# Mem's norm factors from squares of mem^T on GpSimd and two small matmuls, in place of a block of mem squared on ScalarE

## The chip, the core and the metric

The kernel runs on one core of a Trainium2 chip. The metric is the device time of one execution in microseconds (us), lower is better. A core has TensorE (PE, with its weight loads PEld), VectorE (DVE), ScalarE (ACT), GpSimd (POOL) and SyncE (SP), which issues most of the DMAs. Each engine runs its own instructions in order and waits for the others by semaphores.

## What is computed

A trunk of two layers over 256 tokens of width 1024. Each layer normalizes its input, projects it, runs 12 self-attention heads (layer 0 with forget gates, layer 1 with ALiBi) and 4 cross-attention heads into 256 fixed memory tokens `mem`, adds the output projection, and runs a SwiGLU feed-forward block (FFN). Shapes: `x` and `mem` (1, 256, 1024), all float32. What matters here is the part on `mem`:

```
def rms_norm(x, g):
    y = x * lax.rsqrt(jnp.mean(x * x, axis=-1, keepdims=True) + RMS_EPS)
    return y * g

for i in range(2):
    xn = rms_norm(h, norm_mix[i])
    mn = rms_norm(mem, norm_mem[i])
    mkv = mn @ w_mem_kv[i]
    mk, mv = split_heads(mkv[..., :256], 4), split_heads(mkv[..., 256:], 4)
    proj = xn @ (w_in_fox[0] if i == 0 else w_in_moba[0])      # q, k, v, gates (i == 0), qm
    ...
    mem_out = memory_attention(qm, mk, mv)
    ...
```

The factor of a memory token, one over the root of its mean square, is the same in both layers.

## The kernel before

All weights come as one stream of blocks of up to 1 MB, [128 partitions, 2048 columns], in the order in which `Plan` lists them. `fetch` loads the next block into one of four `raw` buffers; `split` makes of half a block at a time a rounded part `hi` (ScalarE, line 215) and a rest `lo` (VectorE, line 216), so that three matmuls (hi x hi, lo x hi, hi x lo; `prod`) stand for one of full precision. Each use of a half splits five halves ahead, and each split fetches up to three blocks ahead.

`x` and `mem` come transposed into the same stream (`xT`, `memT`): channel on the partition, token on the column, eight slices k of 128 channels. `split_x` makes `x_x` and `x_mem` of them, with the gain applied (line 237 on ScalarE, line 238 on VectorE). The norm factors per token aren't needed for the matmuls; they are applied to their results. For that, before the change, `mem` comes a second time, as a block of its own with the token on the partition (`U["mem"]`): `mem_kv(0)` squares it on ScalarE with a running sum (`mean_square`, line 243), adds epsilon on VectorE (`me_mem`, line 254), raises to -1/2 on GpSimd (`rs_mem`, line 256), and `spread` makes a row of the factors for all partitions with four matmuls (`rsb_ps_mem`) and a copy (`rsb_mem`, line 267).

PE's and SP's instructions go out in the order in which the program lists them (`manual_schedule`); those of VectorE, ScalarE and GpSimd are put in order by a planner that runs while the program is built. That program order in layer 0: values and gates (`v_ps`); q and k of the first four heads (`qk_ps`, g = 0); then `memory_heads`: keys and values of the memory tokens (`mk_ps`, `mv_ps`; eight slices k, "mkv" below), the memory queries (`qm_ps`, eight slices k), and q and k of the next heads (g = 1, 2). Attention of a pair of heads is a generator (`attend`) that `step()` moves on between the slices: `s_m` and `s_s` are the scores of memory and self heads, `p_m` and `p_s` the probabilities. `split_queries` and `split_keys` make the operands `xq`, `xk`, `mk`, `xqm` from the scaled products, on ScalarE, VectorE and GpSimd.

`gate_sums` makes the running sums of the gates: two products, a copy `fr`, a DMA to memory (`fd`, line 490) and three DMAs that spread it over all partitions (`fk`, line 493). `bias` makes from `fk` the additive bias of a pair of self heads (line 510). PSUM banks (eight) and the `work` tiles are shared in turn.

Of the kernel before, what the change touches and what calls it, by code (L numbers as in the profile page):

```python
# [20 lines left out]
F32 = mybir.dt.float32  # L21
# [3 lines left out]
ALU = mybir.AluOpType  # L25
# [3 lines left out]
P = 128  # L29
D = 1024  # L30
S = 256
# [47 lines left out]
class Plan:  # L79


    def __init__(self, a):
        self.shapes, self.blocks, self.U = [], [], {}
        U = self.U
        xT = np.ascontiguousarray(a["x"][0].T)
        memT = np.ascontiguousarray(a["mem"][0].T)
        U["xT"] = self.unit([xT], 0, KD, 0, S)
        for i in range(2):
            w = a["w_in_fox"][0] if i == 0 else a["w_in_moba"][0]
            nv = SW + (H if i == 0 else 0)  # L90
            U["vf", i] = []
            for u in range(4):
                U["vf", i].append(self.unit([w], 2 * u, 2, 2 * SW, nv))
            for g in range(3):
                if g == MEM_AT[i]:
                    if i == 0:
                        U["memT", 0] = self.unit([memT], 0, KD, 0, S)
                        self.mkv(a, 0)
                        self.blocks.append(a["mem"][0].reshape(NT, P, D).transpose(1, 0, 2).reshape(-1))
                        self.shapes.append((NT, 1, D))  # L100
                        U["mem"] = len(self.shapes) - 1
                    U["qm", i] = self.unit([w], 0, KD, 2 * SW + nv, MW)
                U["qk", i, g] = [self.unit([w[:, :SW], w[:, SW:]], 4 * u, 4, g * 2 * P, 2 * P) for u in range(2)]
            U["out", i] = [self.unit([a["w_out"][i]], 2 * j, 2, 0, D) for j in (3, 0, 1, 2)]
            U["gu", i], U["dn", i] = {}, {}
            wgu = a["w_gate_up"][i]
            for c in range(NFC):
                U["gu", i][c, 0] = self.gate_up(wgu, 2 * c)
                if c == NFC - 1:
                    U["gu", i][c, 1] = self.gate_up(wgu, 2 * c + 1)  # L110
                if c > 0:
                    U["dn", i][c - 1] = self.unit([a["w_down"][i]], 2 * (c - 1), 2, 0, D)
                if c < NFC - 1:
                    U["gu", i][c, 1] = self.gate_up(wgu, 2 * c + 1)
            U["dn", i][NFC - 1] = self.unit([a["w_down"][i]], 2 * (NFC - 1), 2, 0, D)
            if i == 0:
                U["memT", 1] = self.unit([memT], 0, KD, 0, S)
                self.mkv(a, 1)
# [20 lines left out]
def trunk(ctx: ExitStack, tc: tile.TileContext, plan, stream, x, gains, norm_final, b_fgate, square, out):  # L139
# [40 lines left out]


    U = plan.U
    raw_only = {U["xT"], U["memT", 0], U["memT", 1], U["mem"]}
    halves = [(i, j * (sh[0] // 2), sh[0] // 2) for i, sh in enumerate(plan.shapes) if i not in raw_only for j in range(2)]
    starts = np.concatenate([[0], np.cumsum([P * int(np.prod(sh)) for sh in plan.shapes])])
    ready, raws, counts = {}, {}, [0, 0]
# [100 lines left out]
    def split_x(i, gain, dst, ks=range(KD)):  # L287

        fetch_to(i + 1)
        for k in ks:  # L290
            split_ps(dst[0][:, k, :], dst[1][:, k, :], raws[i][:, k, 0, :], gT[:, k, gain:gain + 1])
# [28 lines left out]
    rs_mem = []  # L320
    rsb_mem = []

    def mem_kv(i):

        xs = xposed(f"mem{i}")
        split_x(U["memT", i], 2 + i, xs, range(MEM_AHEAD))
        yield
        kb, vb = bank(f"mk_ps{i}"), bank(f"mv_ps{i}")
        for u in range(2):
            for kk in range(4):  # L330
                wh, wl = weights(U["mkv", i][u], kk)
                k = 4 * u + kk
                mv_ = (xs[0][:, k, :], xs[1][:, k, :])
                if k + MEM_AHEAD < KD:
                    split_x(U["memT", i], 2 + i, xs, (k + MEM_AHEAD,))
                for p in range(HM // 2):
                    c = slice(p * P, (p + 1) * P)
                    prod(kb, kb.t[:, p * S:(p + 1) * S], (wh[:, 0, c], wl[:, 0, c]), mv_, k == KD - 1)
                for t in range(NT):
                    c = slice(MW, 2 * MW)  # L340
                    prod(vb, vb.t[:, t * S:(t + 1) * S], tok(xs, k, t), (wh[:, 0, c], wl[:, 0, c]), k == KD - 1)
                if kk % 2:
                    yield
        if i == 0:
            fetch_to(U["mem"] + 1)
            rs_mem.extend(factor(raws[U["mem"]][:, t, 0], f"mem{t}") for t in range(NT))
            rsb_mem.append(spread(rs_mem, "mem", (1.0,), "mem")[:, 0, :])
        mk = ap.tile([P, HM // 2, S], F32, tag="work", name=f"mk{i}", bufs=WORK_BUFS)
        nc.vector.tensor_mul(mk, kb.t.rearrange("p (a s) -> p a s", a=2), rsb_mem[0].unsqueeze(1).to_broadcast([P, 2, S]))
        for p in range(HM // 2):  # L350
            split_keys(mks[p], mk[:, p])
        for t in range(NT):
            nc.scalar.activation(mvs[t][:, :, 0:DH], vb.t[:, t * S:(t + 1) * S].rearrange("p (a d) -> p a d", d=DH),
                                 AF.Copy, scale=rs_mem[t])
# [4 lines left out]
    def split_queries(dst, q):  # L359

        for a in range(2):
            nc.scalar.activation(dst[HOME[a], a], q[HOME[a]], AF.Copy)  # L362
        for a in range(2):
            ENG[a].tensor_sub(dst[HOME[1 - a], a], q[HOME[a]], dst[HOME[a], a].bitcast(F32))

    def split_keys(dst, k):

# [63 lines left out]
        yield  # L431

    active = []

    def step():
        for g in list(active):
# [4 lines left out]
    def mixer(i, xs, rs):  # L441
# [41 lines left out]
        def gate_sums():  # L483
            yield
            fb = bank("F_ps")
            fb.mm(fb.t[:H, 0:S], lf[:, 0], prefix)
            fb.mm(fb.t[:H, P:S], lf[:, 1], prefix[:, 0:P], stop=True)
            fr = ap.tile([P, 2, S], F32, tag="work", name="fr", bufs=WORK_BUFS)[:H, 0]
            nc.vector.tensor_copy(fr, fb.t[:H, :S])
            nc.sync.dma_start(fd, fr)  # L490
            for g in range(GATE_PARTS):
                hs = slice(g * (H // GATE_PARTS), (g + 1) * (H // GATE_PARTS))
                nc.sync.dma_start(fk[:, hs], fd[hs].unsqueeze(0).to_broadcast([P, H // GATE_PARTS, S]))
            gb = bank("Fq_ps")
            for t in range(NT):
                for u in range(t + 1):
                    gb.mm(gb.t[:, t * H:(t + 1) * H], prefix[:, (t - u) * P:(t - u + 1) * P], lf[:, u], stop=u == t)
            nc.scalar.activation(fq.rearrange("p t h -> p (t h)"), gb.t[:, :NT * H], AF.Copy)

        def bias(h0):  # L500

            b = fk[:, h0:h0 + 2]
            if i == 1:
                for a in range(2):
                    nc.gpsimd.tensor_scalar(b[:, a], dist, -float(slopes[h0 + a]), NEG, op0=ALU.mult, op1=ALU.max)
                return b[:, :, P:], b
            b0 = ap.tile([P, 2, P], F32, tag="bias", name=f"bias{h0}", bufs=1)
            for a in range(2):
                for t, o in ((0, b0), (1, b)):
                    nc.vector.scalar_tensor_tensor(o[:, a], b[:, a, :(t + 1) * P], fq[:, t, h0 + a:h0 + a + 1], mask[:, P - t * P:],  # L510
                                                   op0=ALU.subtract, op1=ALU.add)
            return b0, b

        hT = xposed(f"hT{i}")
# [2 lines left out]
        def memory_heads():  # L517
            if i == 0:
                g = mem_kv(0)
                next(g)  # L520
                for j in range(4):
                    next(g)
                    step()
            qb = bank(f"qm_ps{i}")
            for k in range(KD):
                wh, wl = weights(U["qm", i], k)
                for p in range(HM // 2):
                    c = slice(p * P, (p + 1) * P)
                    prod(qb, qb.t[:, p * S:(p + 1) * S], (wh[:, 0, c], wl[:, 0, c]), (xs[0][:, k, :], xs[1][:, k, :]), k == KD - 1)
                if k == 3:  # L530
                    step()
            if i == 0:
                next(g, None)
            qm = ap.tile([P, 2, S], F32, tag="work", name=f"qm{i}", bufs=WORK_BUFS)
            nc.vector.tensor_mul(qm, qb.t.rearrange("p (a s) -> p a s", a=2), rsb[:, 0:1, :].to_broadcast([P, 2, S]))
            for p in range(HM // 2):
                xq = ap.tile([P, 2, S], F32R, tag="work", name=f"xqm{i}{p}", bufs=WORK_BUFS)
                split_queries(xq, qm[:, p])
                active.append(attend(f"m{i}{p}", xq, mks[p], mvs, 2 * p, IDLE_MEM[i] + p, None, hT, 6 + p))

        for g in range(3):
# [245 lines left out]
```

## Time and profile before

| | |
|---|---|
| median of three runs | 627.83 us (625.1 to 628.57) |
| the profiled execution's own time | 628.3 us |
| its span, first to last instruction | 626.5 us |
| busy PE, PEld, DVE, ACT, POOL | 97, 86, 73, 63, 10% |
| mean granted TensorE clock | 0.992 of full speed |
| DMA | 112.31 MB, 179 GB/s |

In the rows, a time in front is the start in us from the span's first instruction; an operation is written out<-in by the program's names, without buffer numbers; x2 means that two were merged into one row, with the time from the first one's start to the last one's end. L216 is line 216 of the kernel. `SPq` is SP's issue of a DMA. "[0.9 <-PE x]" is idle time of the engine ahead of the row and what ended it.

### The profile page before, as it was taken

To read this page: it belongs to the slowest core of one execution; us is meant where nothing else is said; L and a number is where in the kernel's file an instruction comes from. 1 tells how busy PE (TensorE), PEld (TensorE's weight loads), DVE (VectorE), ACT (ScalarE), POOL (GpSimd) and SP (SyncE) were. 2 spreads that over 40 slices of the span, in tenths; PEclk is the share of its full clock that TensorE was granted. 3 is DMA by queue.
4 is the path that set the end of the run, shared out by engine and by line. 5 is a ranking of instruction groups with operands and counts; after the bars stand their busy time and mean duration, and the time that the engine had idled before them with its cause. 6 is when DMAs were issued, how large, how long until landed. Compare 5 with 4: busy or idle time off the path is not lost.

```text
span 626.5 us, 9569 instructions
## 1 busy us (share of the span) xinstructions
PE 609.5 (97%) x3636; PEld 536.2 (86%) x3636; DVE 457.3 (73%) x827; ACT 392.6 (63%) x734; POOL 60.4 (10%) x90
## 2 busy tenths in 40 slices
PE   7999899999999999999999999999999999999995
PEld 5999887778888888888899999877888888888884
DVE  5588899978676666668675589986876666676664
ACT  6679887666555555557466589875755555555542
POOL 2021345300000000000011033100000000000000
PEclk8999899999999999999999999999999999999999
DMA  8974812445555555555555633332455545555301
GB/s 293 390 283 166 347 69 85 146 173 202 199 174 179 194 196 202 194 177 176 210 186 194 215 140 126 135 134 68 169 201 202 186 176 181 198 201 202 136 0 67
DMA packets 17638, 112.31 MB, mean 179 GB/s; under 512 B 2220, under 2 KB 2744, under 8 KB 5432
## 3 DMA queue, kind: packets, MB, share of 16 engines
q1 hardware_dynamic: 17304, 111.42, 49.1%
q8 instruction: 28, 0.46, 0.3%
q10 hardware_dynamic: 288, 0.29, 0.1%
q14 instruction: 18, 0.15, 0.1%
HBM read 110.64 MB, written 1.06 MB: 178 GB/s over the span
## 4 chain that ended last, share of the span: by engine, by line
PE 83%; DVE 7%; ACT 6%; issue 2%; DMA 2%; POOL 0%; SPq 0%; POOLq 0%; ACTq 0%; DVEq 0%
PE gu L178 39%; PE d_acc L178 18%; PE qk_ps L178 8%; PE v_ps L178 6%; PE o_acc L178 4%; DVE lo L216 2%; DMA raw<-in_stream 2%; ACT hi L215 2%; PE s_s L178 1%; ACT p_s L406 1%; PE mv_ps L178 1%; PE qm_ps L178 1%; PE mk_ps L178 1%; PE s_m L178 1%; ACT xq L362 1%
## 5 line engine op out<-in xcount | busy, mean ns | idle before, releaser
L216 DVE TENSOR_TENSOR lo<-raw,hi 128x1024 fp32r<-128x1024 f32 (+3 forms) x201 | 240.6, 1204 | 70.6 <-ACT hi L215 65.6
L215 ACT ACTIVATE hi<-raw 128x1024 fp32r<-128x1024 f32 (+3 forms) x201 | 206.2, 1034 | 74.2 <-PE d_acc L178 47.0
L178 PE MATMUL gu<-x_ffn,hi 128*128 128x512 f32 x704 | 177.5, 392 | 0.0
L178 PEld LDWEIGHTS gu<-x_ffn,hi 128*128 128x128 f32 x704 | 126.3, 189 | 22.2
L178 PE MATMUL d_acc<-hi,h 128*128 128x512 f32 x348 | 107.1, 389 | 0.0
L178 PEld LDWEIGHTS gu<-x_ffn,lo 128*128 128x128 f32 x704 | 96.7, 190 | 8.1 <-ACT x_ffn L237 1.0
L178 PE MATMUL gu<-x_ffn,lo 128*128 128x256 f32 x704 | 100.5, 284 | 0.2
L178 PEld LDWEIGHTS d_acc<-hi,h 128*128 128x128 f32 x348 | 65.3, 188 | 13.6
L178 PE MATMUL qk_ps<-x_x,hi 128*128 128x256 f32 x384 | 73.7, 288 | 0.0
L178 PE MATMUL d_acc<-lo,h 128*128 128x512 f32 x174 | 67.7, 389 | 0.0
L178 PEld LDWEIGHTS qk_ps<-x_x,hi 128*128 128x128 f32 x384 | 62.1, 195 | 0.8 <-issue 0.8
L178 PE MATMUL qk_ps<-x_x,lo 128*128 128x256 f32 x192 | 55.0, 286 | 0.0
L642 ACT ACTIVATE gate<-gu 128x256 f32<-128x256 f32 x44 | 16.9, 384 | 57.6 <-PE gu L178 57.6
L178 PE MATMUL o_acc<-hi,x_hT 128*128 128x512 f32 x128 | 41.7, 404 | 0.6 <-DVE x_hT L235 0.3
L642 ACT ACTIVATE up<-gu 128x256 f32<-128x256 f32 x44 | 16.9, 385 | 40.0 <-PE gu L178 39.7
L178 PEld LDWEIGHTS d_acc<-lo,h 128*128 128x128 f32 x174 | 32.7, 188 | 6.8
L178 PEld LDWEIGHTS qk_ps<-x_x,lo 128*128 128x128 f32 x192 | 37.6, 196 | 0.0
L643 DVE TENSOR_TENSOR gate<-gu,gate 128x256 f32<-128x256 f32 x44 | 18.7, 424 | 25.8 <-ACT gate L642 25.8
L643 DVE TENSOR_TENSOR up<-gu,up 128x256 f32<-128x256 f32 x44 | 18.7, 425 | 25.1 <-ACT up L642 25.1
L178 PE MATMUL v_ps<-hi,x_x 128*128 128x384 f32 (+1 forms) x128 | 34.3, 350 | 1.7 <-ACT hi L215 1.7
L406 ACT ACTIVATE p_s<-p_s,nmax_s 128x128 f32<-128x128 f32 (+1 forms) x48 | 21.4, 446 | 11.8 <-DVE nmax_s L396 11.6
L178 PEld LDWEIGHTS o_acc<-hi,x_hT 128*128 128x128 f32 x128 | 22.8, 188 | 6.4 <-issue 1.3
(152 smaller groups left out, 752.3 us busy)
## 6 DMA issues: line engine op xcount, KB each, us to landing
raw<-in_stream SPq DMA_DIRECT2D x95, 1024.0 KB, 4.8
raw<-in_stream SPq DMA_DIRECT2D x4, 768.0 KB, 4.5
raw<-in_stream SPq DMA_DIRECT2D x2, 780.0 KB, 8.3
fk<-fd SPq DMA_DIRECT2D x3, 512.0 KB, 4.9
raw<-in_stream SPq DMA_DIRECT2D x3, 390.0 KB, 6.2
h<-in_x SPq DMA_DIRECT2D x2, 512.0 KB, 7.1
raw<-in_stream SPq DMA_DIRECT2D x1, 512.0 KB, 7.1
gfin<-in_norm_final SPq DMA_DIRECT2D x1, 512.0 KB, 3.7
```

Of the source, the lines that this page charges most:

```text
L178: nc.tensor.matmul(o, lhsT, rhs, start=self.fresh, stop=stop, skip_group_check=True)
L215: nc.scalar.activation(hi[:, c0:c1], src[:, c0:c1], AF.Copy)
L216: nc.vector.tensor_sub(lo[:, c0:c1], src[:, c0:c1], hi[:, c0:c1].bitcast(F32))
L362: nc.scalar.activation(dst[HOME[a], a], q[HOME[a]], AF.Copy)
L406: nc.scalar.activation(pr[:, a, c], src, AF.Exp, bias=nmax[:, a, j], scale=scale, accum_out=total[:, a, j])
L642: nc.scalar.activation(v[:, 1], b[s].t[:, S:], AF.Copy)
L643: nc.vector.tensor_add(v[:, 0], b[s].t[:, :S], v[:, 1])
```

## The change

The block `mem` leaves the stream. In its place GpSimd squares the eight slices of `memT` and adds them up (`mem_squares`), and two matmuls with a column of -1 sum over the partitions, token by token (`mem_factors`); the same two steps on VectorE and GpSimd as before make the factors. These matmuls are issued after slice k = 1 of the memory queries, and `spread` with the scaling of `mk` and `mv` after k = 4 instead of behind all eight. Further: the three DMAs of `fk` are issued two steps later, and the instructions of `bias` are kept behind the last VectorE instruction of the second pair's `split_queries` (`issue_after`: an order on the same engine, no wait).

```
-                        self.blocks.append(a["mem"][0].reshape(NT, P, D).transpose(1, 0, 2).reshape(-1))
-                        self.shapes.append((NT, 1, D))
-                        U["mem"] = len(self.shapes) - 1
...
-    raw_only = {U["xT"], U["memT", 0], U["memT", 1], U["mem"]}
+    raw_only = {U["xT"], U["memT", 0], U["memT", 1]}
...
+    def mem_squares():
+        w = cp.tile([P, 2, S], F32, name="squares")
+        for k in range(KD):
+            src = raws[U["memT", 0]][:, k, 0, :]
+            nc.gpsimd.tensor_mul(w[:, min(k, 1)], src, src)
+            if k > 0:
+                nc.gpsimd.tensor_add(w[:, 0], w[:, 0], w[:, 1])
+        return w[:, 0]
+
+    def mem_factors(sums):
+        b = bank("ms_mem")
+        for t in range(NT):
+            b.mm(b.t[:, 2 * t:2 * t + 2], sums[:, t * P:(t + 1) * P], prefix[:, P:P + 2], stop=True)
+        for t in range(NT):
+            me = sp.tile([P, 1], F32, tag="me", name=f"me_mem{t}")
+            nc.vector.tensor_scalar(me, b.t[:, 2 * t:2 * t + 1], -1.0 / D, EPS, op0=ALU.mult, op1=ALU.add)
+            rs = sp.tile([P, 1], F32, tag="rs", name=f"rs_mem{t}", bufs=8)
+            nc.gpsimd.tensor_tensor(rs, me, minus_half, op=ALU.pow)
+            rs_mem.append(rs)
+
     def mem_kv(i):
         xs = xposed(f"mem{i}")
         split_x(U["memT", i], 2 + i, xs, range(MEM_AHEAD))
+        if i == 0:
+            sums = mem_squares()
         yield
...
         if i == 0:
-            fetch_to(U["mem"] + 1)
-            rs_mem.extend(factor(raws[U["mem"]][:, t, 0], f"mem{t}") for t in range(NT))
+            mem_factors(sums)
+            yield
             rsb_mem.append(spread(rs_mem, "mem", (1.0,), "mem")[:, 0, :])
...
     (split_queries)
         for a in range(2):
-            ENG[a].tensor_sub(dst[HOME[1 - a], a], q[HOME[a]], dst[HOME[a], a].bitcast(F32))
+            r = ENG[a].tensor_sub(dst[HOME[1 - a], a], q[HOME[a]], dst[HOME[a], a].bitcast(F32))
+        return r
...
+    mem_done = {}
...
     (gate_sums)
             nc.sync.dma_start(fd, fr)
-            for g in range(GATE_PARTS):
-                hs = slice(g * (H // GATE_PARTS), (g + 1) * (H // GATE_PARTS))
-                nc.sync.dma_start(fk[:, hs], fd[hs].unsqueeze(0).to_broadcast([P, H // GATE_PARTS, S]))
...
             nc.scalar.activation(fq.rearrange("p t h -> p (t h)"), gb.t[:, :NT * H], AF.Copy)
+            yield
+            yield
+            for g in range(GATE_PARTS):
+                hs = slice(g * (H // GATE_PARTS), (g + 1) * (H // GATE_PARTS))
+                nc.sync.dma_start(fk[:, hs], fd[hs].unsqueeze(0).to_broadcast([P, H // GATE_PARTS, S]))
...
     (bias)
-                    nc.vector.scalar_tensor_tensor(o[:, a], b[:, a, :(t + 1) * P], fq[:, t, h0 + a:h0 + a + 1], mask[:, P - t * P:],
-                                                   op0=ALU.subtract, op1=ALU.add)
+                    with tc.issue_after(mem_done[i]):
+                        nc.vector.scalar_tensor_tensor(...)
...
     (memory_heads, in the loop over k of qm)
+                if i == 0 and k in (1, 4):
+                    next(g, None)
                 if k == 3:
                     step()
-            if i == 0:
-                next(g, None)
...
-                split_queries(xq, qm[:, p])
+                mem_done[i] = split_queries(xq, qm[:, p]).ins
```

## Rows read from the trace of the kernel before

**Rows 1.** The page: busy time and share of the span of each engine, and the chain that ended last by engine.

```profile
PE 609.5 (97%) x3636; PEld 536.2 (86%) x3636; DVE 457.3 (73%) x827; ACT 392.6 (63%) x734; POOL 60.4 (10%) x90
PE 83%; DVE 7%; ACT 6%; issue 2%; DMA 2%; POOL 0%; SPq 0%; POOLq 0%; ACTq 0%; DVEq 0%
```

**Rows 2.** What PE waited for between 40 and 130 us: us in total, times, longest.

```profile
PE s_m L178 <- POOL xqm L364: 2.0, 1, 2.0
...
```

**Rows 3.** The chain that ended last, in order of time (start us, us, what), around that wait.

```profile
...
54.26 5.95 DMA raw<-in_stream
...
66.06 1.22 PE s_m L178 x8
67.28 4.37 PE qk_ps L178 x24
...
72.61 0.94 PE s_m L178 x8
73.56 2.88 PE qk_ps L178 x24
...
```

**Rows 4.** The two squares of mem on ScalarE (line 243) between 40 and 60 us: count, ns min/median/max, first and last start.

```profile
L243 ACT ACTIVATE junk_mem<-raw x2: 1043/1045/1047, 50.2 to 53.1; 128x1024 bf16<-128x1024 f32 x2
```

**Rows 5.** Busy time in some stretches: stretch, its length, then busy us (instructions) of PE, PEld, DVE, ACT, POOL, the granted clock, the DMAs' share and GB/s.

```profile
65.00:70.00 5.00, 3.94 (x22) 3.94 (x23) 4.66 (x10) 4.87 (x11) 1.51 (x2) 0.71 1.04 418
...
85.00:113.00 28.00, 25.99 (x177) 20.75 (x174) 27.33 (x72) 22.58 (x55) 12.24 (x14) 1.00 0.29 110
```

**Rows 6.** VectorE's two `lo` of the qm block (timeline of VectorE), SP's issues of `fd` and `fk` (timeline of SP).

```profile
49.27 2.36 DVE L216 TENSOR_TENSOR lo<-raw,hi 128x1024 fp32r<-128x1024 f32 x2 [1.10 <-ACT hi L215]
...
54.64 0.44 SPq L490 DMA_DIRECT2D fd<-fr  x1
60.39 1.29 SPq L493 DMA_DIRECT2D fk<-fd  x3
```

**Rows 7.** Timeline of PE at the start of mkv, at the start of qm, and at the end of qm with the start of the next q and k.

```profile
38.96 0.28 PE L178 MATMUL mk_ps<-x_mem,lo 128*128 128x256 f32 x1
...
51.97 0.28 PE L178 MATMUL qm_ps<-x_x,hi 128*128 128x256 f32 x1
...
57.73 0.60 PE L178 MATMUL rsb_ps_mem<-sq,rs_mem 128*128 128x128 f32 x4
58.09 0.36 PE L178 MATMUL qk_ps<-x_x,hi 128*128 128x256 f32 x1
```

**Rows 8.** SP's issue of memT's block, and the time from its issue to its landing.

```profile
16.89 0.33 SPq L198 DMA_DIRECT2D raw<-in_stream  x1
...
DMA to landing us min/median/max: 13.9/13.9/13.9
```

**Rows 9.** Timeline of GpSimd: from 20 to 43 us, and at 88 us.

```profile
22.47 1.24 POOL L256 TENSOR_TENSOR rs_x<-me_x,minus_half 128x1 f32<-128x1 f32 x2 [17.67 <-DVE me_x L254]
42.03 1.60 POOL L364 TENSOR_TENSOR xq<-qk,xq 64x256 fp32r<-64x256 f32 x1 [18.32 <-ACT xq L362]
...
88.49 1.71 POOL L364 TENSOR_TENSOR xq<-qk,xq 64x256 fp32r<-64x256 f32 x1 [2.07 <-ACT xq L362]
```

**Rows 10.** Timelines of VectorE and GpSimd where both have two-input instructions, at 88, 108 and 384 us (VectorE's rows first in each).

```profile
88.39 1.22 DVE L216 TENSOR_TENSOR lo<-raw,hi 128x1024 fp32r<-128x1024 f32 x1
89.64 0.84 DVE L364 TENSOR_TENSOR xq<-qk,xq 64x256 fp32r<-64x256 f32 x1
...
108.26 1.65 DVE L216 TENSOR_TENSOR lo<-raw,hi 128x1024 fp32r<-128x1024 f32 x1
...
108.08 0.74 POOL L372 TENSOR_TENSOR xk<-qk,xk 64x256 fp32r<-64x256 f32 x1 [0.15 <-ACT xk L369]
...
383.70 0.55 DVE L410 TENSOR_SCALAR p_m<-p_m,rc_m 128x256 f32<-128x256 f32 x1
...
384.17 0.88 DVE L410 TENSOR_SCALAR p_m<-p_m,rc_m 128x256 f32<-128x256 f32 x1
...
384.18 0.72 POOL L372 TENSOR_TENSOR xk<-qk,xk 64x256 fp32r<-64x256 f32 x1
```

**Rows 11.** GpSimd's one-input instruction `fk<-sq` (line 505): all twelve, ns min/median/max; two of them in GpSimd's timeline, and VectorE's `lo` under them.

```profile
L505 POOL TENSOR_SCALAR fk<-sq x12: 1066/1070/1916, 73.6 to 119.3; 128x256 f32<-128x256 f32 x12
...
96.34 2.47 POOL L505 TENSOR_SCALAR fk<-sq 128x256 f32<-128x256 f32 x2 [2.18 <-issue]
...
96.67 1.22 DVE L216 TENSOR_TENSOR lo<-raw,hi 128x1024 fp32r<-128x1024 f32 x1
```

**Rows 12.** Timeline of VectorE from 30 to 39 us.

```profile
30.77 2.36 DVE L216 TENSOR_TENSOR lo<-raw,hi 128x1024 fp32r<-128x1024 f32 x2 [0.76 <-ACT hi L215]
33.05 3.25 DVE L238 SCALAR_TENSOR_TENSOR x_mem<-raw,gT,x_mem 128x256 fp32r<-128x256 f32 x8
36.22 2.35 DVE L216 TENSOR_TENSOR lo<-raw,hi 128x1024 fp32r<-128x1024 f32 x2
```

**Rows 13.** Timelines of GpSimd and VectorE around the last `xqm`, and the first reader of `bias` on VectorE.

```profile
65.28 1.60 POOL L364 TENSOR_TENSOR xqm<-qm,xqm 64x256 fp32r<-64x256 f32 x2 [1.07 <-ACT xqm L362]
...
66.32 0.85 DVE L510 SCALAR_TENSOR_TENSOR fk<-fk,fq,sq 128x256 f32<-128x256 f32 x1
67.20 0.42 DVE L364 TENSOR_TENSOR xqm<-qm,xqm 64x256 fp32r<-64x256 f32 x1
...
72.17 0.29 DVE L396 CUSTOM_DVE_ANT_0 p_s<-s_s,bias 128x128 f32<-128x128 f32 x1 [0.91 <-PE s_s L178]
```

More of the change, by code (lines that the diff above doesn't have):

```diff
@@ L509, in bias @@
                 for t, o in ((0, b0), (1, b)):
-                    nc.vector.scalar_tensor_tensor(o[:, a], b[:, a, :(t + 1) * P], fq[:, t, h0 + a:h0 + a + 1], mask[:, P - t * P:],
-                                                   op0=ALU.subtract, op1=ALU.add)
+                    with tc.issue_after(mem_done[i]):
+                        nc.vector.scalar_tensor_tensor(o[:, a], b[:, a, :(t + 1) * P], fq[:, t, h0 + a:h0 + a + 1],
+                                                       mask[:, P - t * P:], op0=ALU.subtract, op1=ALU.add)
             return b0, b
```

## The prediction, made before the changed kernel was run

> **What bounds the kernel now.** I read the page first: PE (TensorE) is busy 97% of the span and makes 83% of the chain that ended last [rows 1]. So a change counts only where it makes PE wait, or ends a wait. The view of PE's waits over the stretch in which mem's factors are made shows where it waits [rows 2]: one wait of 2.0 us is by far the longest, `s_m` (scores of the first memory pair) for `xqm` on GpSimd. The chain in order of time says where that came from [rows 3]: a raw block issued at 54.26 landed 5.95 us later, ScalarE stood in its order at that block's `hi`, and the `mk` and `xqm` copies came behind it, so that `s_m` began at 66.06. The reader should see in ScalarE's own rows that the two squares of mem (1.05 us each) stand ahead of this [rows 4], and that the block's issue at 54.26 comes right behind the second (53.1 + 1.05 and the reading of its sum): the buffer that mem's block held is the one it waited for. After the wait the granted clock falls [rows 5]: 0.71 on average in 65 to 70 us, that is, half (1.2 GHz) for a part of it. The chain prices it: `s_m` took 1.22 us where the next pair took 0.94, and 24 `qk_ps` matmuls took 4.37 us where the next 24 took 2.88 [rows 3]. So the wait costs 1.98, and the low clock behind it 0.28 + 1.49 = 1.77: together 3.75 us.
>
> From 85 to 113 us VectorE is the fuller engine (27.33 of 28 us) and the chain runs through it, but it is fed by `s_s`, `s_m` and `qk`, and it had idled 0.91 us when `s_s` gave it `p_s` at 72.17 [rows 13]: it had no backlog then, so a shift of PE there is passed on. The FFN stages behind do not change.
>
> **The change, removed.** The 1 MB mem block, one place in the stream with four buffers; two squares on ScalarE, 2 x 1.05 = 2.1 us. The last `qk` block no longer waits for a square: its buffer is qm's, free when qm's second `lo` ends at about 51.6 [rows 6], so with the same 6 us it would land near 57.7, ahead of 60.29. ScalarE has 2.1 us less to do and no block to wait for ahead of 66.06, more than the 1.98 that `s_m` lacked. The factors also move: `spread` is issued after k = 4 of qm, not after k = 7, three steps of six matmuls at 0.12 us (2.2 us) earlier than its neighbours. I take the whole 3.75 us as gained; the floor is nothing (rival 3).
>
> **Added on PE.** Two matmuls of two columns. Four of `rsb_ps_mem` took 0.36 us (57.73 to 58.09) [rows 7]; two cost 0.2. Nothing covers them, PE is the bound.
>
> **Added on GpSimd.** Fifteen instructions, eight products and seven sums, each 128x256 with both inputs in SBUF. They can start when memT lands: issued at 16.89, 13.9 us to landing, 30.8 [rows 8]. GpSimd is empty from 23.7 to 42.03 [rows 9]. No row shows a two-input GpSimd instruction on 128 partitions; the nearest are `xq`/`xk`, 64x256, 0.72 us undisturbed, and `fk<-sq`, 128x256 with one input, 1.07 [rows 10, 11]. Alone the fifteen would take 15 x 0.8 = 12 us (with 0.08 between) to 17 and be done by 43 to 48, long before PE has done k = 1 of qm (51.97 + 12 x 0.12 = 53.4 [rows 7]). So GpSimd's own time is covered, even when doubled.
>
> What isn't covered is VectorE. The rows of the two engines side by side show that a two-input GpSimd instruction and a VectorE instruction with two inputs in SBUF take turns [rows 9, 10]. `xq` on GpSimd began at 88.49 under a `lo` that ended at 89.61, and ended at 90.20, 0.59 later; VectorE's `xq`, begun at 89.64, took 0.84 where the like `xqm` at 67.20 took 0.42 alone [rows 13]. A `lo` begun at 108.26 under GpSimd's `xk` took 1.65 for 1.22. And where both have more to do, GpSimd gets the next turn: of VectorE's two `p_m` at 383.70 and 384.17 the second took 0.88 while GpSimd's `xk`, begun at 384.18, took its undisturbed 0.72. The Trainium skill says the same of these ports ("SBUF — State Buffer", Who interferes with whom): the pair is an exclusive lock, held for a whole instruction, and the loser blocks fully. The trace agrees for two-input GpSimd instructions; it does not for the one-input `fk<-sq` at 96.34, under which a `lo` at 96.67 took its plain 1.22 [rows 11]; by the rule that `lo` would have been held.
>
> Now where the fifteen fall. From 30.77 VectorE does two `lo`, eight `x_mem` and two `lo` without a gap, all with two SBUF inputs [rows 12]. With turns, a GpSimd instruction comes before each:
> - second `lo`: 0.59 + 1.09 (the `lo` of 108.26 ended 1.09 after GpSimd's end at 108.82) = 1.68 instead of 1.14: +0.54;
> - eight `x_mem`: 0.59 + 0.29 (the like form `fk` at 66.32 ended 0.29 after GpSimd [rows 13]) = 0.88 instead of 0.40: +3.84;
> - the third `lo`: +0.54.
> Sum +4.9 us. The third `lo` is the first half of mkv's weights. It ended at 36.22 + 1.22 = 37.44, and PE's second mkv matmul needs it at 38.96 [rows 7]: slack 1.5. So PE stands 4.9 - 1.5 = 3.4 us at the start of mkv. Everything on PE is queued behind it. The next `lo` is due 2.9 us later and 1.7 behind the third: no second wait. By the one row that shows it, a wait of 1.98 us is followed by a half clock worth 1.77 us; I take it again in full. The low end of this cost is 0: if a GpSimd instruction came only before every third one, +1.5 fits into the slack. The high end takes 1.07 - 0.72 = 0.35 more for each of ten turns: a wait of 6.9. I take the low price for a turn, since the two-input rows at 64 partitions are the same operation and the one-input row is another. A page has a price for 128 partitions: "GPSIMD Engine Reference", § 3.1 of the Trainium skill, gives 4497 ns for an add of 2048 elements, from which an estimate for 256 is 0.56 us. By it a turn is 0.03 shorter and the sum 0.3 us less.
>
> **Moved.** `fk`'s three DMAs go two steps later, past one raw block on SP's queue; before, `fd` was issued at 54.64 (behind the block that waited for the square) and `fk` at 60.39 [rows 6]. `fd` now leaves about 3 us earlier and `fk` can leave when `fd` has landed and qk's first block is split, so I put it at 57 to 60, as before. `bias` now stands behind the last `xqm`; its first reader came at 72.17, five us after that [rows 13]. Cost 0; without this cover the first softmax starts later one for one. memT's buffer is now free only after the eighth product, the fourteenth turn (ten turns to the third `lo`'s 42.4, four more at 0.9 to 1.7), about 47 instead of 36; the block that takes it lands near 53 (6 us as above) and PE needs it at 58 [rows 7]. Cost 0.
>
> **Sum.** The profiled execution took 628.3 (span 626.5, 1.8 around it). 628.3 - 3.75 + 3.4 + 1.77 + 0.2 = 629.9. The median of the three runs is 0.5 lower, so 629.4 us.
>
> **Rivals.**
> 1. *The squares do not hold VectorE up* (planned behind the `x_mem` work, or the turns go to VectorE as under `fk<-sq`). For it: the one-input rows [rows 11]. Against it: every two-input row, and an empty GpSimd at 30.8. Then 628.3 - 3.75 + 0.2 = 624.8, 624.3 on the median's scale; with one turn in two (+2.5, wait 1.0, no low clock) 625.3.
> 2. *GpSimd's 128-partition instruction costs 0.35 more.* For it: 1.07 against 0.72. Against it: other operation. Wait 6.9: 632.9. This is the slower one; it decides from a wait of 5.0 on (1.6 over the forecast, so 0.16 more for each turn), which is where the time passes 631.0.
> 3. *The factors come late and `s_m` waits as before.* After k = 1 the path is VectorE's `me` behind a `lo` (up to 1.22 + 0.3), then two powers (1.24 [rows 9]): 2.8 us against 2.2 until `spread`, so PE could wait 0.6 there, and if ScalarE's `mk` copies still come behind `hi`s nothing of the 3.75 is gained: 629.4 + 3.75 = 633.2. Against it: ScalarE has 2.1 us more room and no block to wait for.
>
> **Numbers.** Forecast 0.44, rival 1 0.28, rival 2 0.16, rival 3 0.12. The range reaches from just under rival 1 to rival 3: 623.8 to 633.2; the likeliest case alone, with a clock that may fall less, is 627.6 to 631. Half a per cent, 3.1 us, is about what a measurement of this kernel can tell from no change. Below 624.7 lies most of rival 1: 0.20. Above 631.0 lie rival 2, most of rival 3: 0.26. Between: 0.54.
>
> **What would show it.** In the profile after: a wait of PE at the second mkv matmul near 39 for a `lo` on VectorE (3.4 us; absent if rival 1); `x_mem` on VectorE near 0.9 us apart instead of 0.40, its GpSimd instructions 0.9 to 1.7 us long; a half clock within some us behind that wait; no wait before `s_m` and a clock of 1.00 behind it. The prediction is wrong if the fifteen run at another time than 31 to 47 us, if `lo` and `x_mem` keep their durations, or if `spread` becomes a wait.

## The result and the profile after

The changed kernel took 629.99 us (median of 12 executions, 629.34 to 631.39) beside 625.69 for the kernel before on the same chip: ratio 1.0057, 95% interval 1.0042 to 1.0072. It is slower, by a little more than the half per cent that the prediction called telling. The prediction said 629.4 us, so its number was close; several of its terms were not. Its profiled execution took 630.54 us with a span of 628.8.

The page after, busy time by engine and the chain by engine, answers to [rows 1]:

```profile
PE 611.1 (97%) x3640; PEld 536.1 (85%) x3640; DVE 461.3 (73%) x827; ACT 391.3 (62%) x730; POOL 76.6 (12%) x105
PE 80%; DVE 10%; DMA 4%; ACT 3%; issue 2%; SPq 1%; POOLq 0%; POOL 0%; DVEq 0%; ACTq 0%
```

GpSimd has 15 instructions and 16.2 us more; VectorE has its 827 instructions still, but they take 4 us longer, and it holds more of the chain. What PE waited for between 30 and 130 us (us in total, times, longest) answers to [rows 2]:

```profile
PE mk_ps L175 <- DVE lo L213: 2.7, 1, 2.7
PE qk_ps L175 <- ACT p_m L428: 1.8, 2, 0.9
```

The wait before `s_m` is gone; a wait at mkv, where the prediction put it, has come, and two waits of 0.9 us behind `s_m` that it did not foresee. VectorE's timeline answers to [rows 12], GpSimd's and PE's stand under it (start us, us, engine):

```profile
29.80 2.36 DVE L213 TENSOR_TENSOR lo<-raw,hi 128x1024 fp32r<-128x1024 f32 x2 [0.77 <-ACT hi L212]
32.08 6.48 DVE L235 SCALAR_TENSOR_TENSOR x_mem<-raw,gT,x_mem 128x256 fp32r<-128x256 f32 x8
38.48 3.29 DVE L213 TENSOR_TENSOR lo<-raw,hi 128x1024 fp32r<-128x1024 f32 x2
...
31.17 2.21 POOL L325 TENSOR_TENSOR squares<-raw 128x256 f32<-128x256 f32 x2 [6.39 <-DMA raw<-in_stream]
33.47 0.80 POOL L327 TENSOR_TENSOR squares<-squares 128x256 f32<-128x256 f32 x1
34.34 0.68 POOL L325 TENSOR_TENSOR squares<-raw 128x256 f32<-128x256 f32 x1
35.10 0.80 POOL L327 TENSOR_TENSOR squares<-squares 128x256 f32<-128x256 f32 x1
...
39.22 1.48 POOL L325 TENSOR_TENSOR squares<-raw 128x256 f32<-128x256 f32 x1
...
40.28 0.39 PE L175 MATMUL mk_ps<-x_mem,lo 128*128 128x256 f32 x1 [2.73 <-DVE lo L213]
```

One `x_mem` falls to every GpSimd instruction: eight take 6.48 us instead of 3.25, and the two `lo` behind them 3.29 instead of 2.35. Turns, as predicted. The clock (stretch, its length, busy us of PE, PEld, DVE, ACT, POOL, granted clock, DMA share, GB/s) answers to [rows 5]:

```profile
41.50:45.00 3.50, 3.50 (x19) 3.50 (x19) 3.50 (x4) 2.48 (x6) 3.34 (x3) 0.51 0.02 5
65.00:70.00 5.00, 5.00 (x44) 5.00 (x43) 2.76 (x7) 4.82 (x10) 2.26 (x3) 1.00 1.03 410
```

PE works at half clock (1.2 GHz) from 41.5 to 45 us, just behind the new wait, and at full clock where the kernel before had fallen to half.

### The profile page after: what moved, and what is told of

Read it like the earlier page. It is cut to its first block, busy times and chain, and to the rows that moved or that the text cites. A ratio compares the mean times of both kernels' runs of the same rounds, so it can differ in the third digit from the quotient of the medians.

```text
span 628.8 us, 9589 instructions
## 1 busy us (share of the span) xinstructions
PE 611.1 (97%) x3640; PEld 536.1 (85%) x3640; DVE 461.3 (73%) x827; ACT 391.3 (62%) x730; POOL 76.6 (12%) x105
## 4 chain that ended last, share of the span: by engine, by line
PE 80%; DVE 10%; DMA 4%; ACT 3%; issue 2%; SPq 1%; POOLq 0%; POOL 0%; DVEq 0%; ACTq 0%
PE gu L175 39%; PE d_acc L175 18%; PE qk_ps L175 5%; PE o_acc L175 5%; DMA raw<-in_stream 4%; DVE lo L213 3%; PE v_ps L175 3%; PE mk_ps L175 2%; PE mv_ps L175 2%; PE qm_ps L175 2%; PE s_s L175 1%; ACT hi L212 1%; ACT p_s L428 1%; DVE x_mem L235 1%; DVE p_s L418 1%
## 5 line engine op out<-in xcount | busy, mean ns | idle before, releaser
L311 POOL MEMSET xk<- 64x256 f32 x24 | 7.4, 307 | 200.1 <-PE d_acc L175 179.0
L253 POOL TENSOR_TENSOR rs_f<-me_f,minus_half 128x1 f32<-128x1 f32 x5 | 2.7, 554 | 223.5 <-DVE me_f L251 223.5
```

What stands on the lines that cost most here:

```text
L253: nc.gpsimd.tensor_tensor(rs, me, minus_half, op=ALU.pow)
L311: nc.gpsimd.memset(dst[HOME[1 - a], a, S:].bitcast(F32), 0.0)
```

## Experiments

Three theories went in. **1:** GpSimd's two-input squares take turns with VectorE in front of mkv. **2:** the moves cost (the order of `bias`), or memT's buffer, which the squares hold longer. **3:** the way to the factors (small matmuls, powers, spread) is late. One execution can also differ from the next in its clock. The expectations below were written run by run and number their theories anew; what each means stands there with it. The diffs are against the changed kernel, with `...` for lines that are not shown.

Medians in us; the ratio and its interval are the record's for the executions of both kernels, not the quotient of the two medians (for e1 that would be 0.9988); the kernel before took 626.4, 626.4 and 626.3 beside them in the three sets of runs:

| run | median (n) | ratio, 95% interval |
|---|---|---|
| e0_before, one execution | 624.85 | |
| e4_moves_only | 624.69 (12) | 0.9980, 0.9966 to 0.9993 |
| e7_spread_only | 624.61 (12) | 0.9980, 0.9965 to 0.9995 |
| e1_no_squares | 625.62 (12) | 0.9998, 0.9986 to 1.0010 |
| e6_hold_only | 625.61 (12) | 0.9994, 0.9982 to 1.0006 |
| e8_hold_long | 625.89 (11) | 0.9998, 0.9988 to 1.0008 |
| e9_half_squares | 627.37 (8) | 1.0022, 1.0006 to 1.0038 |
| e5_bias_free | 630.00 (6) | 1.0064, 1.0042 to 1.0087 |
| e10_after | 629.93 (5) | 1.0066, 1.0054 to 1.0079 |
| e3_late_squares | 631.67 (4) | 1.0088, 1.0071 to 1.0106 |
| e2_one_input | 634.56 (4) | 1.0137, 1.0113 to 1.0162 |

**The kernel before, once more (e0_before).**

> The kernel before, unchanged, for a second profile. Its runs lie in two groups, 624.5 to 626.5 us and 627.8 to 628.6, and the profile that the prediction read is of the second. If the groups come from the clock, an execution of the first group shows one half-clock stretch fewer (1.7 us each) than the two at 9 to 12.5 us and 67 to 70.5 us; if they come from the waits, the stretches stay and PE's wait before s_m (2.0 us) is gone.

It took 624.85 us, 3.4 less than the profiled execution that the prediction was built on. PE's row at the wait (timeline):

```profile
64.02 0.38 PE L178 MATMUL s_m<-mk,xqm 128*128 128x256 f32 x1 [2.10 <-POOL xqm L364]
```

The stretch behind it (columns as above):

```profile
65.00:70.00 5.00, 5.00 (x44) 5.00 (x44) 4.94 (x16) 4.28 (x13) 0.74 (x2) 1.00 1.01 426
```

The same wait of 2.1 us, and no half clock behind it: 1.00 where [rows 5] have 0.71. So the low clock doesn't belong to the wait as a fixed price. The stretch from 5 to 15 us, which had 0.83 in the profile before (first row), has 1.00 here too (second row):

```profile
5.00:15.00 10.00, 8.25 (x34) 7.05 (x33) 6.23 (x12) 6.88 (x13) 0.00 (x0) 0.83 1.00 369
5.00:15.00 10.00, 9.58 (x46) 8.31 (x45) 7.13 (x13) 7.45 (x13) 0.00 (x0) 1.00 1.03 395
```

**The moves alone (e4_moves_only)** keep mem's block and ScalarE's squares, and all that the change moves (the lines that put the block back into the stream are left out):

```diff
-        if i == 0:
-            sums = mem_squares()
...
-            mem_factors(sums)
+            fetch_to(U["mem"] + 1)
+            rs_mem.extend(factor(raws[U["mem"]][:, t, 0], f"mem{t}") for t in range(NT))
```

> The kernel with mem's block and the two squares on ScalarE as before, and all the moves of the change: factors after k = 1 and k = 4 of qm, fk two steps later, bias behind the last xqm. Theory 1: no wait at mkv, and as the factors come earlier the wait before s_m is short or gone: 622 to 626. Theory 2 (the moves make VectorE late): about as slow as the changed kernel, 628 to 631.

**The spread's move alone (e7_spread_only)** is e4 with `fk`'s DMAs back behind `fd` and no `issue_after` on `bias`.

> The kernel before with one move of the change alone: the spread of mem's factors (the step of mem_kv behind the block of mem) inside the loop over qm instead of behind it; the block of mem and its squares on ScalarE, the DMAs of fk right behind fd, and the order of bias as before. If the earlier spread is all of the gain that the moves gave (624.7): 624 to 625.5, and no wait before s_m. If the order of fk and bias is needed for it (nmax_m stands behind bias and two lo on VectorE): the wait at s_m goes, but p_m is later and PE waits at the second qk_ps by 1 to 2 us more: 625.5 to 627, no better than before.

Both took the same time, 1.7 to 1.8 us less than the kernel before: moving `spread` into the loop over qm is all of the gain, and both beat both kernels. What PE waited for in e7 from 30 to 130 us:

```profile
PE qk_ps L178 <- ACT p_m L430: 0.9, 1, 0.9
PE s_s L178 <- DVE pT_s L445: 0.8, 1, 0.8
PE pT_m L441 <- DVE nmax_s L420: 0.8, 1, 0.8
```

The 2.1 us before `s_m` are gone, and 1.7 come back as two waits (`p_m`, `nmax_s`) that e0_before does not have. With no half clock near these waits in either, e7's span is 622.6 and e0_before's 623.1: half a microsecond is left.

The rest of the 1.8 between the medians goes with the clock, by the mean granted clock that is on record for every execution. Of the 64 executions of the kernel before beside these runs, the 23 with 0.996 or more took 624.6 to 625.7 us (median 625.0), the 41 with 0.995 or less 625.9 to 628.4 (median 626.8). Of e7's twelve, nine have 0.996 or more (median 624.4), of e4's twelve eleven (624.7). So at a like clock the move gains 0.3 to 0.6 us, and the rest is that fewer executions have the lower clock. That it is the wait before `s_m` that makes them fall is not shown: where the clock fell is known only of the profiled executions, and e0_before has the wait without it.

**No squares (e1_no_squares).** One GpSimd memset in place of the fifteen; the factors are not computed from mem.

```diff
-        for k in range(KD):
-            src = raws[U["memT", 0]][:, k, 0, :]
-            nc.gpsimd.tensor_mul(w[:, min(k, 1)], src, src)
-            if k > 0:
-                nc.gpsimd.tensor_add(w[:, 0], w[:, 0], w[:, 1])
+        nc.gpsimd.memset(w[:, 0], 8.0)
```

> The kernel after, with the fifteen GpSimd instructions replaced by one GpSimd memset that reads nothing of memT: memT's buffer is freed by VectorE as before, the two small matmuls, the moves and everything else stay; the factors are not computed from mem. Both theories of the loss (1: VectorE's x_mem and lo take turns with the two-input squares; 2: memT's buffer is held until 47.3 us, so the blocks behind it come late and VectorE pays twice) expect the wait of 2.7 us at mkv, the half clock behind it and the two later waits of 0.9 us to go: 624 to 625 us, as with the moves alone (624.7). If the small matmuls, the two pow or the order of the spread cost something by themselves, it stays above 626.

625.6: the squares are worth 4.4 us of the changed kernel's time, the wait at mkv is gone, the two waits for `p_m` are not:

```profile
PE qk_ps L175 <- ACT p_m L424: 1.8, 2, 0.9
```

It lies 1.0 above e7, and PE's timelines show where, e1 first, then e7:

```profile
51.29 0.51 PE L175 MATMUL ms_mem<-sq,squares 128*128 128x2 f32 x4
51.65 0.36 PE L175 MATMUL qm_ps<-x_x,hi 128*128 128x256 f32 x1
...
53.77 0.28 PE L175 MATMUL qm_ps<-x_x,hi 128*128 128x256 f32 x1
54.09 1.00 PE L175 MATMUL rsb_ps_mem<-sq,rs_mem 128*128 128x128 f32 x4
54.85 0.36 PE L175 MATMUL qm_ps<-x_x,hi 128*128 128x256 f32 x1
```

```profile
53.45 0.28 PE L178 MATMUL qm_ps<-x_x,hi 128*128 128x256 f32 x1
53.57 0.60 PE L178 MATMUL rsb_ps_mem<-sq,rs_mem 128*128 128x128 f32 x4
53.93 0.36 PE L178 MATMUL qm_ps<-x_x,hi 128*128 128x256 f32 x1
```

`ms_mem` takes 0.36 us of PE (51.29 to 51.65). From the last qm matmul before the spread to the first behind it are 54.85 - 53.77 = 1.08 in e1 and 0.48 in e7: 0.6 more, since PE now gets there before the powers. Together 0.96.

**One-input instructions (e2_one_input):** as many GpSimd instructions on the same tiles, each with one input; the factors are not computed from mem.

```diff
-            nc.gpsimd.tensor_mul(w[:, min(k, 1)], src, src)
+            nc.gpsimd.tensor_scalar(w[:, min(k, 1)], src, 1.0, 8.0, op0=ALU.mult, op1=ALU.max)
...
-                nc.gpsimd.tensor_add(w[:, 0], w[:, 0], w[:, 1])
+                nc.gpsimd.tensor_scalar(w[:, 0], w[:, 1], 1.0, 8.0, op0=ALU.mult, op1=ALU.max)
```

> The changed kernel with the fifteen GpSimd instructions in a one-input form (a multiply by 1 with a maximum, 128x256) in place of the products and sums; the factors of mem are therefore not computed. The order on PE, VectorE, ScalarE and SyncE is that of the changed kernel. Theory 1 (GpSimd's two-input instructions take turns with VectorE's x_mem and lo and so make PE wait at the start of mkv): x_mem 0.40 us apart instead of 0.80, no wait of PE at the second mkv matmul, no half clock behind it: 2.7 + 1.7 us less, 625.5 to 626.5. Theory 2 (VectorE's order behind 68 us sets the time, the wait at 38 us is absorbed): within 1 us of 630. Theory 3 (memT's buffer is held up to 47 us and the blocks behind it come late): 630 or more, as the one-input form is longer.

VectorE's timeline, at mkv and where it idled longest:

```profile
31.50 3.67 DVE L235 SCALAR_TENSOR_TENSOR x_mem<-raw,gT,x_mem 128x256 fp32r<-128x256 f32 x8
...
55.12 2.36 DVE L213 TENSOR_TENSOR lo<-raw,hi 128x1024 fp32r<-128x1024 f32 x2 [8.04 <-ACT hi L212]
```

Its GpSimd instructions that stand for the products (ns min/median/max, first and last start):

```profile
L325 POOL TENSOR_SCALAR squares<-raw x8: 1067/1262/1797, 29.4 to 48.1; 128x256 f32<-128x256 f32 x8
```

PE's longest wait:

```profile
PE rsb_ps_mem L175 <- POOL rs_mem L339: 8.6, 1, 8.6
```

SP's next issues of raw blocks (timeline of SP):

```profile
49.18 2.08 SPq L195 DMA_DIRECT2D raw<-in_stream  x4
```

Theory 1 holds at its place: the eight `x_mem` take 3.67 us under busy GpSimd, not 6.48, and PE doesn't wait at mkv. So it is not a busy GpSimd as such that makes VectorE take turns, but the two-input form; as the operation changed with the number of inputs, that it is the second input alone is argued. But the time is worse, by what theories 2 and 3 name together: these instructions are longer, hold memT's buffer until 49.2, the raw blocks come late, VectorE idles 8.04 us, `me` stands behind its next `lo`, and PE waits 8.6 us for the powers.

**Half the squares (e9_half_squares):** the first four of eight blocks, seven instructions; the factors come from half of mem.

```diff
-        for k in range(KD):
+        for k in range(KD // 2):
```

> The kernel after with the squares of the first four of the eight 128x256 blocks only (seven GpSimd instructions instead of fifteen; the factors come from half of mem). By the rows of after the seven run from 31.2 to 36.7 us, so six or seven x_mem still take 0.80 us each, the last one or two and the two lo run undisturbed. Turns with VectorE: the lo that PE waits for ends at 32.1 + 6 x 0.80 + 2 x 0.40 + 1.14 = 38.9 instead of 40.2, PE waits 1.4 us instead of 2.7 at mkv, and 626.9 (625.6 + 1.3) without a half clock, 628.7 with one. If the loss came from how long memT's buffer is held, it would be all gone: 625.6.

PE's wait, and VectorE's timeline:

```profile
PE mk_ps L175 <- DVE lo L213: 1.4, 1, 1.4
```

```profile
31.46 5.42 DVE L235 SCALAR_TENSOR_TENSOR x_mem<-raw,gT,x_mem 128x256 fp32r<-128x256 f32 x8
36.80 2.35 DVE L213 TENSOR_TENSOR lo<-raw,hi 128x1024 fp32r<-128x1024 f32 x2
```

The wait is 1.4 us as the turns give it, and the median 627.4 lies between the two figures that theory 1 gave (626.9 and 628.7), not at the 625.6 of the buffer: the wait goes with the number of turns.

**The buffer (e6_hold_only, e8_hold_long)** is held by tiny GpSimd copies out of memT's block before and behind memsets that read nothing; the factors are not computed from mem. e8:

```diff
...
+        for n in range(2):
+            nc.gpsimd.tensor_copy(w[:, n, :KD], raws[U["memT", 0]][:, :, 0, 0])
+        for n in range(40):
+            nc.gpsimd.memset(w[:, n % 2], 8.0)
+        nc.gpsimd.tensor_copy(w[:, 1, :KD], raws[U["memT", 0]][:, :, 0, 0])
...
```

> The kernel after without its squares, but with memT's buffer held by GpSimd about as long: a tiny copy out of the block when it lands, 48 memsets that read nothing (0.31 us each by the rows of GpSimd's memsets, some 15 us), and a tiny copy out of the block again. The factors are not computed from mem. Theory 1: no instruction with two inputs on GpSimd, so no wait at mkv and no half clock behind it: 624 to 625.5. Theory 2: the raw blocks are issued near 47 us as in the kernel after, VectorE idles some 2.4 us before 61 and PE waits for ScalarE's p_m twice, 1.8 us in all: 626 to 627.5. If a memset holds VectorE up as well, the x_mem show it with 0.6 us and more instead of 0.47.

> The kernel after without its squares, memT's buffer held by GpSimd until about 47.5 us, as long as in the kernel after (in the run with 48 memsets the program order let half of them run before the block had landed, and the buffer was free at 40.9): two tiny copies out of the block when it lands, 40 memsets of 0.37 us from one to the next (14.8 us), a tiny copy out of the block. The factors are not computed from mem. If the held buffer costs nothing (the squares' turns with VectorE are all of the 4.4 us between the kernel after and the run without squares): 625.6, and PE waits only where that run waits. If it costs: the raw blocks issued at 46.5 to 47.4 land at 51 to 59, ScalarE waits for them near 49 to 52, lo of qm come late, and the time is 626.5 to 628.

In both the last copy came earlier than meant: in e6 half of the memsets ran before the block had landed, in e8 GpSimd was through by 42.5 (timelines of GpSimd and of SP's queue):

```profile
42.19 0.28 POOL L327 COPY squares<-raw 128x8 f32<-128x8 f32 x1
...
42.50 0.80 SPq L195 DMA_DIRECT2D raw<-in_stream  x2
```

Held to 40.9 or 42.5, the buffer costs nothing against e1 (625.6 and 625.9). What a hold up to the 46.4 us of the changed kernel (45.3 in e10_after) costs was not measured alone; e10_after's rows below bear on it. The two waits for `p_m` stand in e1 as well, where nothing is held, so they are not its price; where they come from stays open.

**The order of bias (e5_bias_free):** the changed kernel without `issue_after`.

```diff
-                    with tc.issue_after(mem_done[i]):
-                        nc.vector.scalar_tensor_tensor(o[:, a], b[:, a, :(t + 1) * P], ...
+                    nc.vector.scalar_tensor_tensor(o[:, a], b[:, a, :(t + 1) * P], ...
```

> The changed kernel without the order that holds bias behind the last xqm; all else kept. Theory 1: the wait at mkv stays (2.5 to 3 us) and the time is within 1 us of the changed kernel's 630. Theory 2: bias is done while VectorE idles in 60 to 68 us, the first nmax_m starts up to 1.7 us (four bias instructions) earlier than 72.1, and the time falls by 1 to 2 us.

Its wait at mkv:

```profile
PE mk_ps L175 <- DVE lo L213: 3.2, 1, 3.2
```

630.0, as the changed kernel: the order of `bias` costs nothing.

**Squares later (e3_late_squares):** one tiny GpSimd copy makes the squares wait for the first `lo` of mkv (one product still ran ahead of it, at 29.73).

```diff
+        nc.gpsimd.tensor_copy(w[:, 0, 0:1], after)
...
+                if (i, k) == (0, 0):
+                    sums = mem_squares(wl[:, 0, 0:1].bitcast(F32))
```

> The kernel after, with the same fifteen two-input squares, but behind one tiny GpSimd copy that waits for the first lo of mkv's weights, so that they start near 36.6 us, when the eight x_mem are past, and end near 52 to 53. Theory 1 (the lock in front of mkv is the loss): the 2.7 us at mkv and the half clock go, the later lo are stretched to 1.6 but each has slack: 624.5 to 626.5. Theory 2 (the held buffer is the loss): memT's buffer is freed some 5 us later than in the kernel after, at about 52, three raw blocks are issued that much later, VectorE idles 6 us and more and PE waits for it near 56 to 66: 632 to 636.

Neither figure came. PE's row at its wait and GpSimd's last sum (timeline), then the stretch behind the wait:

```profile
56.08 1.01 PE L175 MATMUL ms_mem<-sq,squares 128*128 128x2 f32 x4 [4.76 <-POOL squares L328]
...
54.44 1.59 POOL L328 TENSOR_TENSOR squares<-squares 128x256 f32<-128x256 f32 x1
```

```profile
53.20:60.00 6.80, 3.92 (x18) 3.92 (x19) 2.47 (x4) 0.75 (x1) 5.22 (x6) 0.50 0.66 252
```

The wait at mkv is gone, as theory 1 says. But the turns cost GpSimd as well: under a `lo` a square takes 1.5 to 1.6 us, the last ends at 56.0, not at 52 to 53, PE waits 4.8 us for it at `ms_mem`; the clock falls during that wait (0.50 from 53.2 on), and PE works at half clock up to 60. Moving the squares moves the loss.

**The changed kernel, once more (e10_after).**

> The kernel after, unchanged, a second time beside the others: 629.5 to 630.5, the wait of 2.7 us at mkv again. Open is whether the half clock follows the wait here too (then the time stays near 630.0) or not (then this execution is near 628.3).

It has the wait at mkv and, this time, no half clock behind it, but a wait at the spread (stretch as above, then PE's timeline):

```profile
41.50:45.00 3.50, 3.50 (x31) 3.50 (x30) 3.47 (x4) 2.87 (x6) 3.34 (x3) 1.00 0.00 0
```

```profile
39.77 0.39 PE L175 MATMUL mk_ps<-x_mem,lo 128*128 128x256 f32 x1 [2.56 <-DVE lo L213]
...
58.12 1.01 PE L175 MATMUL rsb_ps_mem<-sq,rs_mem 128*128 128x128 f32 x4 [1.04 <-POOL rs_mem L339]
```

PE, not slowed, comes to the spread before the powers are done and waits 1.04 us. In the first profile the half clock had covered that; its PE at the same place:

```profile
58.79 0.28 PE L175 MATMUL qm_ps<-x_x,hi 128*128 128x256 f32 x1
59.11 1.01 PE L175 MATMUL rsb_ps_mem<-sq,rs_mem 128*128 128x128 f32 x4
59.87 0.36 PE L175 MATMUL qm_ps<-x_x,hi 128*128 128x256 f32 x1
```

From the row at mkv to `ms_mem` PE took 16.03 us there (40.28 to 56.31) and 14.55 here (39.77 to 54.32), so the half clock cost 1.5. Is the 1.04 the price of memT's buffer, held to 45.3 here? VectorE's timeline ahead of `me` says no:

```profile
51.20 0.53 DVE L394 TENSOR_TENSOR xk<-qk,xk 64x256 fp32r<-64x256 f32 x1
51.76 4.63 DVE L213 TENSOR_TENSOR lo<-raw,hi 128x1024 fp32r<-128x1024 f32 x4
56.31 0.22 DVE L337 TENSOR_SCALAR me_mem<-ms_mem 128x1 f32<-128x1 f32 x2
```

VectorE did not wait for a late block there: it works without a gap from 38.09 on. Its four `lo` start 4.0 us later than in e1 (51.76 for 47.73), PE's `ms_mem` only 3.0 (54.32 for 51.29); the difference is the 1.04. It is VectorE's work behind mkv, stretched by more turns, that makes `me` late. (In the first profile a late block did cost VectorE 0.48 us of idle time, at 52.45, but nothing of it reached PE: 59.87 - 58.79 = 1.08 at the spread, as in e1.) So the two executions differ in span by 628.8 - 627.6 = 1.2 only.

## Why the prediction was right, and where it wasn't

On medians of the runs, the change is 626.4 - 1.8 (the spread's move, e7) + 1.0 (small matmuls and the powers' delay, e1 less e7) + 4.4 (the squares, after less e1) = 630.0. The prediction had the three parts with the right signs, and sizes whose errors nearly cancelled; that its sum came within 0.6 us is partly luck. Executions with a mean clock of 0.996 or more alone give 625.0 - 0.6 + 1.2 + 3.8 = 629.4 (five of the changed kernel): there the move is worth a third of what the medians say, and the whole loss is 4.4.

- **The base and the gain of 3.75: mis-sized.** That `s_m` would no longer wait was right. Its cause was put first on the block and the squares of mem; e7 keeps both and has lost the wait, so the earlier `spread` is enough. "I take the whole 3.75 us as gained" was not right: e7 keeps 1.8 on the medians and 0.6 at a like clock, since waits for `p_m` and `nmax_s` take 1.7 of the 2.1 back. The 1.77 for the low clock were read from one execution as if the wait had caused them; e0_before has the wait without them. The 628.3 it was subtracted from held two such half-clock stretches; the median of all later executions of the kernel before lies 1.4 below the 627.8 it was scaled to. A base too high and a gain too large hid each other.
- **The new wait of 3.4: right in place and cause, 2.7 and 2.6 in size.** Of the +4.9 for VectorE, the `lo` at 30.94 was not held (+0.54 expected), since the squares began at 31.17; the eight `x_mem` got 6.48 - 3.25 = +3.23 for +3.84; the next `lo` +0.5 as expected. The slack was 1.1, not 1.5: in the profile before, the half clock at 9 to 12.5 us held PE back, and here PE was ready at 40.28 - 2.73 = 37.55, 1.4 us earlier, where VectorE began 1.0 earlier (29.80 for 30.77). So 3.7 - 1.1 = 2.6. There was no second wait at mkv, as expected.
- **1.77 for a half clock behind it: not a fixed price.** It came in the first profile (0.51 from 41.5 to 45, worth 1.5) and in e5's (0.50 from 41 to 43), not in e10's, where 1.04 at the spread took its place.
- **0.2 for the two matmuls: too small, and a term left out.** The two matmuls are four records of two columns, which took 0.36, as much as the four of 128 columns in [rows 7]; and the powers make PE wait 0.6 in e1, the wait that rival 3 named for `spread` and the sum had left out.
- **Moves at no cost: right.** e4, e5 and e7 show it for `fk` and `bias`, e6 and e8 for memT's buffer up to 42.5 us; beyond that only e10's rows speak for it.
- **Rival 1** (the squares don't hold VectorE) falls with e2 and e9; e2 shows it for one input only, as [rows 11] had it. **Rival 2** (0.35 more for 128 partitions) falls: a two-input square of 128x256 took 0.67 to 0.80 on its turns. **Rival 3** came true in its small part, at the spread (0.6 us in e1, 1.04 more in e10), not at `s_m`.

The lock that the prediction took from the Trainium skill ("SBUF — State Buffer", Who interferes with whom) is what these runs show for two inputs; for one input the rule would hold every `x_mem` up, and e2's median was 0.475 us beside 0.48 in the kernel before, so there the measurement decides. The estimate of 0.56 us for an addition from "GPSIMD Engine Reference", § 3.1 of the Trainium skill, was low: 0.79 to 0.80 on its turns, 0.74 alone (e3).

## What to carry to other kernels

Work put on an idle engine is not free when its instructions take turns with those of a busy one: count the instructions of the busy engine that stand in front of the bound engine's next need, and give each a turn. When a wait is found at the head of a low clock, look at a second execution before the clock is booked with the wait. And when an earlier step turns out to be the gain, as the moved `spread` here, it can be had without the rest of the change: e7_spread_only took 0.2% less than the kernel before (interval 0.05 to 0.35%; most of it by executions with a higher clock) and some 0.9% less than the changed one (624.61 beside 629.99).

## What the hardware showed that I had not expected

- A one-input GpSimd instruction with two operations (`tensor_scalar`, 128x256) took 1.07 us and more, median 1.26; the two-input product or sum of the same size 0.61 to 0.81 when no `lo` ran beside it. Fewer inputs, with one operation more, were dearer.
- A two-input GpSimd instruction held a two-input VectorE instruction up (0.83 to 0.96 us for an `x_mem` of 0.48), a one-input `tensor_scalar` hardly (0.47 to 0.62), a memset not at all (0.47 in e8).
- The same wait of PE (2.1 us before `s_m`, 2.6 to 2.7 at mkv) was followed by half clock in one execution and not in another of the same program.
